# Three float32r products for the attention scores, and linear-attention products grouped by tile shape, in a two-layer trunk

## The chip, the cores and the metric

The kernel runs on one core of a Trainium2 chip. The metric is device time of one execution in microseconds (us).

## What is computed

The reference is a trunk of two layers on 256 tokens of width 1024. Each layer normalises its input, projects it, and feeds three mixers: differential attention (4 heads, two score maps each, c = 0 and 1), a state-space mixer, and gated linear attention (GLA, 4 heads, chunks of 64 tokens). Their outputs are projected and added, and a gated feed-forward part and a gated per-layer input follow. Cut to what the change touches:

```python
# differential attention, one block of 128 query rows
s = jnp.einsum('bqhcd,bkhcd->bhcqk', qi, k) * scale      # d = 64
s = jnp.where(causal, s, -jnp.inf)
pr = jax.nn.softmax(s, axis=-1)
attn = pr[:, :, 0] - lam * pr[:, :, 1]
# gated linear attention
gk = jax.nn.log_sigmoid(gate_lr @ w_gate2 + b_gate) / GLA_GATE_NORMALIZER
o_intra = jnp.einsum('bchls,bcshv->bclhv', att, vf)
states = jnp.einsum('bclhd,bclhv->bchdv', k_end, vf)     # per chunk of 64
o_inter = jnp.einsum('bclhd,bchdv->bclhv', q_dec, prev)  # prev: state before the chunk
o = rms_norm(o_intra + o_inter, g_norm) * silu(g_out)
```

All inputs and outputs are float32.

## The kernel before

Every large product is made of float32r products. `load_w` brings a weight tile by DMA into a staging buffer, rounds it on ScalarE (ACT) into a high part `wh` (L212) and subtracts on VectorE (DVE) to get the low part `wl` (L213); operands are split in the same way, and a product is high x high, high x low, low x high (`product` L225 to L227, `product_t` L237 to L245, the x units L824 to L826). The small products in the mixers have float32 operands; TensorE (PE) executes such a matmul as two records in the trace.

The work of a layer is a list of weight units. `PLAN` and `PLAN_OUT` say at which unit a generator of the mixers makes its next step: `da_gen` (differential attention), `ssd_gen` (state space), `gla_gates_gen` and `gla_gen` (GLA). The order on each engine is then set by a scheduler from priorities and dependencies. The weight units need five banks of PSUM (`bank_acc`, name acc); all mixer steps share three (`bank`, name pm). A fourth tile of pm waits until the readers of the first have ended. There are six halves of weight buffers (`NHALF`), so splits run up to three weight tiles ahead.

In `da_gen`, q and k are turned by PE transposes (L430) and copied by ACT into `qt` (L433). The scores come in three groups: the first 128 rows with 4 heads and 128 keys, and the second 128 rows with two times 2 heads and 256 keys. Each head and c has one float32 product with K = 64 (c = 0 in array rows 0 to 63, c = 1 in rows 64 to 127; L458) and then one bfloat16 product of 128 columns that adds the causal mask (L460). DVE takes the row maxima `mx` (L466), ACT the exponentials `e` (L471). The products of the state-space mixer behind the first scores are L602; DVE adds them to `xd` (L605), and the scales of L615 follow.

In GLA, `lrx` holds the low-rank gate input with a column of ones, its transpose `lrt` is multiplied with the gate weights (L694, float32). `gla_gen` forms the attention map `pa` (L726, masked into `attm` by DVE L728), turns k (L732), makes three chunk states (L744, K = 64, float32, one bank for each chunk), copies them with decay into `gst` (L757 and below), and then makes the outputs `po`: for each j, b and e one 128x128 product with `attm` (L770) and up to two 64x64 products with the states (L776). A head norm on ACT and DVE (L373 to L380), a gate (L785, writing `fyn`) and transposes (L793) follow.

Of the kernel before, what the change touches and what calls it, by code (L numbers as in the profile page):

```python
# [10 lines left out]
F32 = mybir.dt.float32  # L11
# [5 lines left out]
ALU = mybir.AluOpType  # L17
# [90 lines left out]
def trunk_kernel(ctx: ExitStack, tc: tile.TileContext, a: dict):  # L108
# [15 lines left out]
    def slot(s, dt=F32):  # L124
        return sp.tile([P, SLOT], dt, tag="slot", name=nm(s))
# [29 lines left out]
    for b in range(2):  # L155
        pool.memset(lrx[b], 0.0)
        pool.memset(lrx[b][:, 16:17], 1.0)
# [237 lines left out]
    def da_gen(i, S):  # L395
# [30 lines left out]
        for t in range(4):  # L426
            pb = bank()
            for hh in range(2):
                for b in range(2):
                    pe.transpose(pb[:, (2 * hh + b) * P:(2 * hh + b + 1) * P],  # L430
                                 qg[t][:, b * T + hh * P:b * T + (hh + 1) * P], ident)
            qt = slot("qt")
            act.activation(qt, pb, AF.Copy)  # L433
            qk.append(qt)
            if t == 1:
                yield
# [13 lines left out]
        for qb, heads in units:  # L450
            nh, nk = len(heads), P * (qb + 1)
            pb = [bank(), bank()]
            for j, hd in enumerate(heads):
                q, k = qk[hd // 2], qk[2 + hd // 2]
                o = (hd % 2) * T
                for c in range(2):
                    r = slice(64 * c, 64 * c + 64)
                    pe.matmul(pb[c][:, j * nk:(j + 1) * nk], q[r, o + qb * P:o + (qb + 1) * P],  # L458
                              k[r, o:o + nk], start=True, stop=False)
                    pe.matmul(pb[c][:, (j + 1) * nk - P:(j + 1) * nk], idb, negb, start=False, stop=True)  # L460
# [221 lines left out]
    def gla_gates_gen(i, S):  # L682

        wt = slot("w2")
        pool.dma_start(wt[:, :256], a["w2"][i])
        pl = bank()
        for b in range(2):
            pe.transpose(pl[:, b * P:(b + 1) * P], lrx[b], ident)
        lrt = slot("lrt")
# [3 lines left out]
        for b in range(2):  # L693
            pe.matmul(pg[:, b * T:(b + 1) * T], lrt[:, b * P:(b + 1) * P], wt[:, :256], start=True, stop=True)  # L694
# [19 lines left out]
    def gla_gen(i, S):  # L714
# [24 lines left out]
        pst = []  # L739
        for c in range(3):  # L740
            b, r = c // 2, slice(64 * (c % 2), 64 * (c % 2) + 64)
            pb = bank()
            for j in range(2):
                pe.matmul(pb[:, j * T:(j + 1) * T], kx[r, (2 * b + j) * P:(2 * b + j + 1) * P],  # L744
                          v[b][r, j * T:(j + 1) * T], start=True, stop=True)
            pst.append(pb)
# [16 lines left out]
        po = [bank(), bank()]  # L763
        for j in range(2):
            for b in range(2):
                o = (2 * j + b) * P
                for e in range(2):
                    hd = 2 * j + e
                    r = slice(64 * e, 64 * e + 64)
                    pe.matmul(po[e][:, o:o + P], attm[e][:, 2 * j + b], v[b][:, hd * P:(hd + 1) * P],  # L770
                              start=True, stop=True)
                    for cc in range(2):
                        c = 2 * b + cc
                        if c:
                            s = j * T + b * P + cc * 64
                            pe.matmul(po[e][64 * cc:64 * cc + 64, o:o + P], q[r, s:s + 64],  # L776
                                      prev[c][r, j * P:(j + 1) * P], start=False, stop=True,
                                      skip_group_check=True)
# [29 lines left out]
    def in_units(i, S, x):  # L808
# [45 lines left out]
        def zunit(half):  # L854
            def go(w):
# [4 lines left out]
                for b in range(2):  # L860
# [7 lines left out]
                    else:  # L868
                        dve.tensor_scalar(lrx[b][:, 0:16], pb[:, T:T + 16], rcol[:, b:b + 1], None,
                                          op0=ALU.mult)  # L870
# [234 lines left out]
def _layout(w):  # L1105
# [23 lines left out]
    w2[:, 0:16] = z["gla_w_gate2"]  # L1129
    w2[:, 16] = z["gla_b_gate"]  # L1130
# [44 lines left out]
```

## Time and profile before

| | us |
|---|---|
| median of 3 runs | 809.76 |
| lowest and highest run | 808.99, 810.79 |
| the profiled execution, device time | 808.72 |
| its span in the trace | 806.7 |
| its mean granted TensorE clock | 0.991 of full speed |
| busy: PE, DVE, ACT | 796.1, 624.6, 472.8 |

The span is the time between first and last instruction of the trace; the device time has 2 us around it. Busy time of PE counts matmuls and not weight loads (PEld), which run beside them. The granted clock is the share of full speed (2.4 GHz) that PE was given; 0.5 is 1.2 GHz. Of each timeline, the ends of matmuls are modelled, so the distance from one start to the next is what a matmul costs, and not its duration.

### The profile page before, as it was taken

How to read it: one execution, taken by the hardware profiler on the slowest of the kernel's cores; microseconds unless marked ns; L12 is line 12 of the kernel's file. 1: busy time of each engine (PE TensorE's matmuls, PEld its weight loads, DVE VectorE, ACT ScalarE, POOL GpSimd, SP SyncE). 2: the span in 40 equal slices, each digit the busy share in tenths (PEclk: the TensorE clock that was granted, in tenths of full speed). 3: DMA queues.
4: the chain of work that ended last, by engine and by line, in shares of the span. 5: the costliest groups of instructions: out<-in, count | busy, mean ns of one | idle time of the engine just before them, and what ended most of it. 6: DMA issues, size and time to landing. Idle time of an engine off the chain costs nothing.

```text
span 806.7 us, 13118 instructions
## 1 busy us (share of the span) xinstructions
PE 796.1 (99%) x5026; PEld 703.7 (87%) x5026; DVE 624.6 (77%) x1279; ACT 472.8 (59%) x820; POOL 22.8 (3%) x34
## 2 busy tenths in 40 slices
PE   8999999999999999999999999999999999999997
PEld 6998876899888888888999987778998888888897
DVE  5998977788787777667789699777888777766673
ACT  7767556556665555455667675284566566555461
POOL 2000000002000000000010000000020000000000
PEclk9999989999999999999999999899999999999999
DMA  8764331444655544557554532333445555445541
GB/s 295 278 213 140 139 103 54 157 157 158 209 164 203 188 162 144 179 182 247 207 206 163 177 112 99 107 135 124 158 160 198 197 180 206 138 153 191 196 157 53
DMA packets 24013, 134.92 MB, mean 167 GB/s; under 512 B 2960, under 2 KB 4752, under 8 KB 11408
## 3 DMA queue, kind: packets, MB, share of 16 engines
q1 hardware_dynamic: 23616, 133.57, 48.3%
q8 instruction: 39, 0.64, 0.3%
q0 software_dynamic: 192, 0.52, 0.2%
q14 instruction: 22, 0.18, 0.1%
q10 hardware_dynamic: 144, 0.01, 0.0%
HBM read 133.05 MB, written 1.05 MB: 166 GB/s over the span
## 4 chain that ended last, share of the span: by engine, by line
PE 91%; DVE 3%; ACT 2%; DMA 2%; issue 1%; SPq 0%; DVEq 0%; ACTq 0%
PE acc L237 30%; PE acc L239 15%; PE acc L245 7%; PE acc L244 7%; PE acc L243 7%; PE acc L824 4%; PE acc L825 4%; PE acc L826 4%; PE pm L458 2%; PE pm L602 1%; DMA h<-in_x 1%; PE acc L226 1%; PE acc L225 1%; PE acc L227 1%; DVE wl L213 1%
## 5 line engine op out<-in xcount | busy, mean ns | idle before, releaser
L212 ACT ACTIVATE wh<-st 128x1024 fp32r<-128x1024 f32 (+5 forms) x274 | 267.4, 979 | 234.6 <-PE acc L237 91.3
L213 DVE TENSOR_TENSOR wl<-st,wh 128x1024 fp32r<-128x1024 f32 (+5 forms) x274 | 309.3, 1132 | 105.1 <-ACT wh L212 104.8
L237 PE MATMUL acc<-x,wh 128*128 128x512 f32 x704 | 222.0, 396 | 0.1
L239 PEld LDWEIGHTS acc<-x,wl 128*128 128x128 f32 x704 | 132.3, 188 | 31.2
L239 PE MATMUL acc<-x,wl 128*128 128x256 f32 x704 | 138.4, 278 | 0.0
L237 PE MATMUL acc<-act,wh 128*128 128x512 f32 x352 | 111.8, 395 | 0.0
L237 PEld LDWEIGHTS acc<-x,wh 128*128 128x128 f32 x704 | 107.3, 189 | 0.7 <-DVE x L274 0.7
L245 PE MATMUL acc<-x,wl 128*128 128x256 f32 x320 | 90.7, 283 | 0.9 <-DVE wl L213 0.9
L243 PE MATMUL acc<-x,wh 128*128 128x256 f32 x320 | 90.9, 284 | 0.0
L244 PE MATMUL acc<-x,wh 128*128 128x256 f32 x320 | 90.5, 283 | 0.0
L239 PEld LDWEIGHTS acc<-act,wl 128*128 128x128 f32 x352 | 66.2, 188 | 14.3
L239 PE MATMUL acc<-act,wl 128*128 128x256 f32 x352 | 72.0, 279 | 0.0
L824 PE MATMUL acc<-wh,x 128*128 128x512 f32 x160 | 66.3, 417 | 0.5 <-ACT wh L212 0.5
L825 PE MATMUL acc<-wl,x 128*128 128x512 f32 x160 | 65.1, 407 | 0.0
L826 PE MATMUL acc<-wh,x 128*128 128x512 f32 x160 | 64.4, 403 | 0.0
L245 PEld LDWEIGHTS acc<-x,wl 128*128 128x128 f32 x320 | 61.2, 191 | 1.1 <-DVE wl L213 1.1
L243 PEld LDWEIGHTS acc<-x,wh 128*128 128x128 f32 x320 | 61.2, 191 | 0.2
L244 PEld LDWEIGHTS acc<-x,wh 128*128 128x128 f32 x320 | 61.2, 191 | 0.1
L237 PEld LDWEIGHTS acc<-act,wh 128*128 128x128 f32 x352 | 54.9, 189 | 1.3
L244 PE MATMUL acc<-mix,wh 128*128 128x256 f32 x192 | 54.6, 285 | 0.0
L243 PE MATMUL acc<-mix,wh 128*128 128x256 f32 x192 | 54.3, 286 | 0.0
L245 PE MATMUL acc<-mix,wl 128*128 128x256 f32 x192 | 54.1, 283 | 0.0
(259 smaller groups left out, 1167.8 us busy)
## 6 DMA issues: line engine op xcount, KB each, us to landing
st<-in_w_f SPq DMA_DIRECT2D x44, 1024.0 KB, 4.9
st<-in_w_d SPq DMA_DIRECT2D x32, 704.0 KB, 4.1
st<-in_w_x SPq DMA_DIRECT2D x18, 1024.0 KB, 4.9
st<-in_w_o SPq DMA_DIRECT2D x12, 1024.0 KB, 4.9
st<-in_w_t SPq DMA_DIRECT2D x11, 1024.0 KB, 4.9
st<-in_w_g SPq DMA_DIRECT2D x8, 1024.0 KB, 5.0
st<-in_w_z SPq DMA_DIRECT2D x3, 1088.0 KB, 5.0
st<-in_w_x SPq DMA_DIRECT2D x8, 256.0 KB, 4.8
```

The source lines that it names most:

```text
L212: i_hi = act.activation(wh[:, s], st[:, o], AF.Copy)
L213: i_lo = dve.tensor_tensor(wl[:, s], st[:, o], wh[:, s].bitcast(F32), ALU.subtract)
L225: pe.matmul(out, sh, mh, start=i == 0, stop=False)
L237: pe.matmul(out, wh[:, lo:lo + P], x[k], start=k == 0, stop=False)
L239: pe.matmul(out[:, :T], wl[:, lo:lo + P], x[k][:, :T], start=False, stop=k == n - 1)
L243: pe.matmul(out, sh, hi, start=k == 0, stop=False)
L244: pe.matmul(out, sh, x[k][:, T:], start=False, stop=False)
L245: pe.matmul(out[:, :T], sl, hi, start=False, stop=k == n - 1)
L458: pe.matmul(pb[c][:, j * nk:(j + 1) * nk], q[r, o + qb * P:o + (qb + 1) * P], k[r, o:o + nk], start=True, stop=False)
L824: pe.matmul(pb[b], xh, wh, start=kk_ == 0, stop=False)
L825: pe.matmul(pb[b], xh, wl, start=False, stop=False)
L826: pe.matmul(pb[b], xl, wh, start=False, stop=kk_ == KD - 1)
```

## The change

It does four things in each layer.

- **Scores.** q and k are kept in two parts, `qh` (ACT copy, rounded to float32r) and `ql` (DVE, what is left of the value in PSUM, 128x512, four per layer). Each head and c has three float32r products with K = 64 (high x high, high x low, low x high, c alternating inside), 48 per layer in place of 16 float32 ones. The mask is one bfloat16 product for a whole bank (6 per layer in place of 16).
- **Gates.** `lrx` holds the high part at columns 0 and 32 and the low part at 64 (and ones at 16 and 48); the gate weights are repeated at rows 0, 32 and 64, of which 32 to 63 are turned into their low part. One float32r product does what a float32 one did. It adds one ACT copy of 128x256, a DVE subtraction of 32x256, and two small DVE operations for each half of the tokens.
- **States.** The loops are exchanged: j outside, the three chunks inside, the three banks taken first.
- **Outputs.** In `po` all products with `attm` come first, then all with the states.

```diff
--- before.py
+++ after.py
@@ -154,7 +154,8 @@
     lrx = [cp.tile([P, P], F32, name=f"lrx{b}") for b in range(2)]
     for b in range(2):
         pool.memset(lrx[b], 0.0)
-        pool.memset(lrx[b][:, 16:17], 1.0)
+        for o in (16, 48):
+            pool.memset(lrx[b][:, o:o + 1], 1.0)
     attm = [cp.tile([P, 4, P], F32, name=f"attm{e}") for e in range(2)]
     for e in range(2):
         (pool if e else dve).memset(attm[e], 0.0)
@@ -429,9 +430,11 @@
                 for b in range(2):
                     pe.transpose(pb[:, (2 * hh + b) * P:(2 * hh + b + 1) * P],
                                  qg[t][:, b * T + hh * P:b * T + (hh + 1) * P], ident)
-            qt = slot("qt")
-            act.activation(qt, pb, AF.Copy)
-            qk.append(qt)
+
+            qh, ql = slot("qh", F32R), slot("ql", F32R)
+            act.activation(qh, pb, AF.Copy)
+            dve.tensor_tensor(ql, pb, qh.bitcast(F32), ALU.subtract)
+            qk.append((qh, ql))
             if t == 1:
                 yield
         yield
@@ -453,11 +456,17 @@
             for j, hd in enumerate(heads):
                 q, k = qk[hd // 2], qk[2 + hd // 2]
                 o = (hd % 2) * T
-                for c in range(2):
-                    r = slice(64 * c, 64 * c + 64)
-                    pe.matmul(pb[c][:, j * nk:(j + 1) * nk], q[r, o + qb * P:o + (qb + 1) * P],
-                              k[r, o:o + nk], start=True, stop=False)
-                    pe.matmul(pb[c][:, (j + 1) * nk - P:(j + 1) * nk], idb, negb, start=False, stop=True)
+
+                for n, (a_, b_) in enumerate(((0, 0), (0, 1), (1, 0))):
+                    for c in range(2):
+                        r = slice(64 * c, 64 * c + 64)
+                        pe.matmul(pb[c][:, j * nk:(j + 1) * nk], q[a_][r, o + qb * P:o + (qb + 1) * P],
+                                  k[b_][r, o:o + nk], start=j == 0 and n == 0, stop=False,
+                                  skip_group_check=True)
+            for c in range(2):
+
+                pe.matmul(v3(pb[c], nh)[:, :, nk - P:], idb, negb.unsqueeze(1).to_broadcast([P, nh, P]),
+                          start=False, stop=True, skip_group_check=True)
             if len(es_of) == 2:
                 attn_t(es_of[0])
             mx = small("mx", [P, 2, 4])
@@ -681,17 +690,20 @@
 
     def gla_gates_gen(i, S):
 
-        wt = slot("w2")
+        wt, wr = slot("w2"), slot("w2r", F32R)
         pool.dma_start(wt[:, :256], a["w2"][i])
+        act.activation(wr[:, :256], wt[:, :256], AF.Copy)
+        dve.tensor_tensor(wr[32:64, :256], wt[32:64, :256], wr[32:64, :256].bitcast(F32), ALU.subtract)
         pl = bank()
         for b in range(2):
             pe.transpose(pl[:, b * P:(b + 1) * P], lrx[b], ident)
-        lrt = slot("lrt")
+        lrt = slot("lrt", F32R)
         act.activation(lrt[:, :T], pl[:, :T], AF.Copy)
         yield
         pg = bank()
         for b in range(2):
-            pe.matmul(pg[:, b * T:(b + 1) * T], lrt[:, b * P:(b + 1) * P], wt[:, :256], start=True, stop=True)
+
+            pe.matmul(pg[:, b * T:(b + 1) * T], lrt[:, b * P:(b + 1) * P], wr[:, :256], start=True, stop=True)
         e = slot("ge")
         act.activation(e, pg, AF.Abs)
         act.activation(e, e, AF.Exp, scale=-1.0)
@@ -736,14 +748,12 @@
         yield
 
         v = S["gv"]
-        pst = []
-        for c in range(3):
-            b, r = c // 2, slice(64 * (c % 2), 64 * (c % 2) + 64)
-            pb = bank()
-            for j in range(2):
-                pe.matmul(pb[:, j * T:(j + 1) * T], kx[r, (2 * b + j) * P:(2 * b + j + 1) * P],
+        pst = [bank() for _ in range(3)]
+        for j in range(2):
+            for c in (0, 1, 2):
+                b, r = c // 2, slice(64 * (c % 2), 64 * (c % 2) + 64)
+                pe.matmul(pst[c][:, j * T:(j + 1) * T], kx[r, (2 * b + j) * P:(2 * b + j + 1) * P],
                           v[b][r, j * T:(j + 1) * T], start=True, stop=True)
-            pst.append(pb)
         prev = [None]
         for c in range(3):
             st = slot("gst")
@@ -761,21 +771,23 @@
             prev.append(st)
         yield
         po = [bank(), bank()]
+
         for j in range(2):
             for b in range(2):
                 o = (2 * j + b) * P
                 for e in range(2):
                     hd = 2 * j + e
+                    pe.matmul(po[e][:, o:o + P], attm[e][:, 2 * j + b], v[b][:, hd * P:(hd + 1) * P],
+                              start=o == 0, stop=False, skip_group_check=True)
+        for j in range(2):
+            for c in range(1, 4):
+                b, cc = c // 2, c % 2
+                o, s = (2 * j + b) * P, j * T + c * 64
+                for e in range(2):
                     r = slice(64 * e, 64 * e + 64)
-                    pe.matmul(po[e][:, o:o + P], attm[e][:, 2 * j + b], v[b][:, hd * P:(hd + 1) * P],
-                              start=True, stop=True)
-                    for cc in range(2):
-                        c = 2 * b + cc
-                        if c:
-                            s = j * T + b * P + cc * 64
-                            pe.matmul(po[e][64 * cc:64 * cc + 64, o:o + P], q[r, s:s + 64],
-                                      prev[c][r, j * P:(j + 1) * P], start=False, stop=True,
-                                      skip_group_check=True)
+                    pe.matmul(po[e][64 * cc:64 * cc + 64, o:o + P], q[r, s:s + 64],
+                              prev[c][r, j * P:(j + 1) * P], start=False, stop=True,
+                              skip_group_check=True)
         ys, sg = [], S["sg"]
         for e in range(2):
             yn = head_norm(po[e])
@@ -866,8 +878,12 @@
                         dve.scalar_tensor_tensor(S["dtr"][:, b], pb[:, T:T + 8], rcol[:, b:b + 1],
                                                  pr[:, O_DTB:O_DTB + 8], ALU.mult, ALU.add)
                     else:
-                        dve.tensor_scalar(lrx[b][:, 0:16], pb[:, T:T + 16], rcol[:, b:b + 1], None,
-                                          op0=ALU.mult)
+
+                        lr, hi = small("lr", [P, 16]), lrx[b][:, 0:64].rearrange("p (a c) -> p a c", a=2)
+                        dve.tensor_scalar(lr, pb[:, T:T + 16], rcol[:, b:b + 1], None, op0=ALU.mult)
+                        dve.tensor_copy(hi[:, :, 0:16].bitcast(F32R),
+                                        lr.unsqueeze(1).to_broadcast([P, 2, 16]))
+                        dve.tensor_tensor(lrx[b][:, 64:80], lr, lrx[b][:, 0:16], ALU.subtract)
                 if half == 1:
                     S["dt"], S["dta"] = ssd_dt(i, S["dtr"])
             made[f"z{half}"] = (a["w_z"][i, half], KD, 272, go)
@@ -1126,8 +1142,9 @@
     out["pos"] = pos.view(np.int32).reshape(2, P, -1).transpose(1, 0, 2)
     cw = z["ssd_conv_w"].reshape(DEPTH, 4, 8, P).transpose(0, 3, 2, 1).reshape(DEPTH, P, 32)
     w2 = np.zeros((DEPTH, P, 256), f)
-    w2[:, 0:16] = z["gla_w_gate2"]
-    w2[:, 16] = z["gla_b_gate"]
+    for r in (0, 32, 64):
+        w2[:, r:r + 16] = z["gla_w_gate2"]
+        w2[:, r + 16] = z["gla_b_gate"]
     out["par"] = np.concatenate([
         cols(z["attn_norm"], 8), cols(z["ffn_norm"], 8), cw, cols(z["ssd_conv_b"], 8),
         cols(z["ssd_norm"], 4), cols(z["gla_norm"], 1), cols(z["da_sub_norm"], 1),
```

Line numbers after the change are some 10 higher: L458 becomes L463, L460 L468, L602 L611, L744 L755, L770 L780, L776 L788, L793 L805, L728 L740, L466 L475, L605 L614, L213 L214.

The order on the engines changes more than the lines say. It is the same in both layers; the rows are those of the first.

PE, the state products (`kx`, L744 before, L755 after). Before, they stand in one piece, 24 wide projections (128x512) behind L602:

```order
L824 MATMUL acc_1412<-wh_1245,x_146 128x512
L825 MATMUL acc_1412<-wl_1246,x_146 128x512
L826 MATMUL acc_1412<-wh_1245,x_146 128x512
L744 MATMUL pm_1447<-gv_1322,kx_1268 128x256 x2
L744 MATMUL pm_1450<-gv_1322,kx_1268 128x256 x2
L744 MATMUL pm_1453<-gv_1323,kx_1268 128x256 x2
L824 MATMUL acc_1411<-wh_1327,x_156 128x512
L458 MATMUL pm_1471<-qt_1289,qt_1275 128x256
L460 LDWEIGHTS idb
L460 MATMUL pm_1471<-negb,idb 128x128
```

After, they are three pieces with projections between them, and the second scores follow at once:

```order
L838 MATMUL acc_1441<-wh_1256,x_148 128x512
L755 MATMUL pm_1476<-gv_1341,kx_1279 128x256 x2
L836 MATMUL acc_1440<-wh_1346,x_158 128x512
L837 MATMUL acc_1440<-wl_1347,x_158 128x512
L838 MATMUL acc_1440<-wh_1346,x_158 128x512
L755 MATMUL pm_1477<-gv_1341,kx_1279 128x256 x2
L836 MATMUL acc_1441<-wh_1346,x_158 128x512
L837 MATMUL acc_1441<-wl_1347,x_158 128x512
L755 MATMUL pm_1478<-gv_1342,kx_1279 128x256 x2
L463 MATMUL pm_1500<-qh_1304,qh_1286 128x256
L463 MATMUL pm_1500<-ql_1305,qh_1286 128x256
L463 MATMUL pm_1500<-qh_1304,ql_1287 128x256
```

Between the products of L602 (L611 after) and the first of them stand 24 wide projections before and 10 after; between the transposes of k (L732, L744 after) and the first scores, 17 before and 30 after. The scores of the first rows (L463) stand together, c alternating, with one of them three projections ahead of the rest; in the second rows each bank's six products and its mask stand apart, one c at a time. The first piece of L755 takes the bank that the products L611 held; what frees it is the addition to `xd` on DVE, which reads them.

DVE, up to that addition (`xd_914<-pm_1379` before, `xd_925<-pm_1408` after). Before, two weight splits (`wl`) stand between the second masking of GLA's map (`attm`) and the row maxima `mx`:

```order
L728 COPY_PREDICATED attm_87<-cst,pm_1252 128x512
L190 TENSOR_TENSOR rs_t_1168<-yf_1166 128x2
L213 TENSOR_TENSOR wl_1328<-st_1326,wh_1327 128x1024
L191 SCALAR_TENSOR_TENSOR rs_t_1168<-rs_t_1168,rs_v_1167 128x2
L213 TENSOR_TENSOR wl_1333<-st_1326,wh_1332 128x1024
L192 SCALAR_TENSOR_TENSOR yf_1166<-rs_t_1168,yf_1166 128x2
L466 TENSOR_REDUCE mx_1354<-pm_1336 128x4
L615 TENSOR_SCALAR xd_886<-xd_886,yf_1166 128x256 x2
L466 TENSOR_REDUCE mx_1354<-pm_1337 128x4
L605 TENSOR_TENSOR xd_914<-pm_1379,xd_914 128x512
L467 TENSOR_SCALAR mx_1354<-mx_1354 128x8
L213 TENSOR_TENSOR wl_1439<-st_1437,wh_1438 128x1024
```

After, four `ql` follow the masking, of which the last two are shown, and behind the scales of `xd` there are five weight splits:

```order
L436 TENSOR_TENSOR ql_1305<-pm_1299,qh_1304 128x512
L193 SCALAR_TENSOR_TENSOR yf_1177<-rs_t_1179,yf_1177 128x2
L436 TENSOR_TENSOR ql_1314<-pm_1308,qh_1313 128x512
L624 TENSOR_SCALAR xd_897<-xd_897,yf_1177 128x256 x2
L214 TENSOR_TENSOR wl_1347<-st_1345,wh_1346 128x1024
L214 TENSOR_TENSOR wl_1352<-st_1345,wh_1351 128x1024
L214 TENSOR_TENSOR wl_1468<-st_1466,wh_1467 128x1024
L214 TENSOR_TENSOR wl_1473<-st_1466,wh_1472 128x1024
L214 TENSOR_TENSOR wl_1563<-st_1561,wh_1562 128x1024
L475 TENSOR_REDUCE mx_1383<-pm_1355 128x4
L475 TENSOR_REDUCE mx_1383<-pm_1356 128x4
L614 TENSOR_TENSOR xd_925<-pm_1408,xd_925 128x512
```

The five splits have moved ahead of the maxima of the scores, and the addition to `xd` stands behind both.

PE, the output products of GLA. Before, the two kinds alternate over both banks (`pm_1681` and `pm_1682`), in eight rounds:

```order
L770 MATMUL pm_1681<-gv_1322,attm_86 128x128
L776 MATMUL pm_1681<-gst_1456,gq_760 64x128
L770 MATMUL pm_1681<-gv_1323,attm_86 128x128
L776 MATMUL pm_1681<-gst_1461,gq_760 64x128
L770 MATMUL pm_1682<-gv_1322,attm_87 128x128
L776 MATMUL pm_1682<-gst_1456,gq_760 64x128
```

After, each bank has four products with `attm` and then six with the states (here from the third):

```order
L780 MATMUL pm_1722<-gv_1341,attm_88 128x128
L780 MATMUL pm_1722<-gv_1342,attm_88 128x128
L788 MATMUL pm_1722<-gst_1485,gq_768 64x128
L788 MATMUL pm_1722<-gst_1490,gq_768 64x128
L788 MATMUL pm_1722<-gst_1495,gq_768 64x128
```

The second bank follows 17 projections of 256 columns later. Behind the products of the second bank, 45 projections stand ahead of the transposes of its normed rows (L805); before, 67 stood ahead of them.

## Rows read from the trace of the kernel before

**Rows 1.** The page, part 1: busy time and share of the span per engine.

```profile
PE 796.1 (99%) x5026; PEld 703.7 (87%) x5026; DVE 624.6 (77%) x1279; ACT 472.8 (59%) x820; POOL 22.8 (3%) x34
```

**Rows 2.** Busy by stretch: span, then PE, PEld, DVE, ACT, POOL busy, PEclk, DMA, GB/s.

```profile
57.00:80.00 23.00, 22.00 (x134) 19.16 (x133) 20.90 (x44) 16.38 (x23) 0.10 (x1) 1.00 0.47 161
80.00:104.00 24.00, 24.00 (x155) 20.79 (x154) 22.79 (x70) 13.43 (x24) 0.00 (x0) 1.00 0.36 127
104.00:109.15 5.15, 5.15 (x33) 3.46 (x31) 4.18 (x9) 2.81 (x5) 0.00 (x0) 1.00 0.17 19
109.15:116.00 6.85, 6.85 (x26) 6.08 (x26) 4.74 (x9) 2.56 (x15) 0.00 (x0) 0.50 0.34 139
505.10:512.00 6.90, 6.90 (x27) 6.05 (x27) 4.53 (x9) 1.96 (x11) 0.00 (x0) 0.51 0.37 141
```

**Rows 3.** Timeline of PE, first scores: start us, duration us, instructions (xcount).

```profile
105.03 0.48 PE L458 MATMUL pm<-qt,qt 64*128 64x128 f32 x2
...
109.03 3.51 PE L602 MATMUL pm<-xdt,m 128*128 128x64 f32 x16
```

**Rows 4.** Timeline of PE, state products and second row block's scores.

```profile
119.12 0.39 PE L825 MATMUL acc<-wl,x 128*128 128x512 f32 x1
119.35 0.39 PE L826 MATMUL acc<-wh,x 128*128 128x512 f32 x1
119.67 1.99 PE L744 MATMUL pm<-gv,kx 64*128 64x256 f32 x12
121.59 0.50 PE L824 MATMUL acc<-wh,x 128*128 128x512 f32 x1
122.02 0.70 PE L458 MATMUL pm<-qt,qt 64*128 64x256 f32 x2
...
123.48 0.48 PE L825 MATMUL acc<-wl,x 128*128 128x512 f32 x1
...
130.57 0.70 PE L458 MATMUL pm<-qt,qt 64*128 64x256 f32 x2
...
132.90 0.61 PE L445 MATMUL pm<-cst,e 128*128 128x128 f32 x4
```

**Rows 5.** Timeline of PE, output products of the linear attention.

```profile
145.72 0.38 PE L770 MATMUL pm<-gv,attm 128*128 128x128 f32 x2
...
147.16 0.49 PE L770 MATMUL pm<-gv,attm 128*128 128x128 f32 x2
147.58 0.43 PE L776 MATMUL pm<-gst,gq 64*64 64x128 f32 x4
147.95 0.49 PE L770 MATMUL pm<-gv,attm 128*128 128x128 f32 x2
...
151.86 0.65 PE L445 MATMUL pm<-cst,e 128*128 128x128 f32 x4
```

**Rows 6.** Timeline of PE, two projections of 256 columns.

```profile
156.06 0.28 PE L226 MATMUL acc<-pl,wh 128*128 128x256 f32 x1
156.18 0.28 PE L227 MATMUL acc<-ph,wl 128*128 128x256 f32 x1
```

**Rows 7.** Groups by line and form: gate product, busy us and mean ns.

```profile
L694 PE MATMUL pm<-w,lrt 128*128 128x256 f32 x8 | 2.1, 378 | 0.0
```

**Rows 8.** Timeline of DVE around the first scores; in brackets idle before, releaser.

```profile
104.48 0.75 DVE L728 COPY_PREDICATED attm<-cst,pm 128x512 f32<-128x512 uint32 x1
...
105.16 1.24 DVE L213 TENSOR_TENSOR wl<-st,wh 128x1024 fp32r<-128x1024 f32 x1
106.30 0.18 DVE L191 SCALAR_TENSOR_TENSOR rs_t<-rs_t,rs_v 128x2 f32<-128x2 f32 x1
...
109.27 0.61 DVE L615 TENSOR_SCALAR xd<-xd,yf 128x256 f32<-128x256 f32 x2
...
112.58 0.69 DVE L605 TENSOR_TENSOR xd<-pm,xd 128x512 f32<-128x512 f32 x1 [2.11 <-PE pm L602]
```

**Rows 9.** Waits of PE: line, released by, us in total, times, longest.

```profile
PE pm L793 <- DVE fyn L785: 0.7, 2, 0.3
```

## The prediction

> **What bounds the kernel.** I read the page's busy times first: PE is busy for 796.1 of 806.7 us, so there is hardly a wait to remove, and any gain must be PE work that goes away [rows 1]. The second view is the busy time by stretch, around the mixers of the first layer [rows 2]. It shows two more things. DVE has little room ahead of the first scores: 2.1 us idle in 57 to 80 and 1.2 us in 80 to 104. And right behind the first scores of each layer PE is granted 0.5 of its clock, 1.2 GHz, for 6.85 us (109.15 to 116) and 6.9 us (505.1 to 512). PE was busy for all 5.15 us ahead of the first fall, so it fell behind short products and not behind an idle engine. At half speed such a stretch costs about 3.4 us. The third view is the timeline, of PE for prices and of DVE for who comes late.
>
> **PE work per layer.** Prices are distances between starts.
>
> *Scores of the first rows.* Before: from 105.03 to 109.03, 4.0 us [rows 3]. After: 24 products of 128 columns and two masks of 512. No row shows a float32r product with K = 64 or under 256 columns; one of 256 columns costs 0.12 us [rows 6], so at most that, unless short ones are priced like float32. The float32 products show that the halves of the array can work side by side: the state products before are twelve records in 1.92 us [rows 4], where two records of 256 columns in a gate product mean 0.52 us (four products in 2.1 us of two layers [rows 7]), so twelve in a row would need 3.1. Here c alternates, so I take twelve pairs at 0.11, 1.3 us, the masks at 0.23 each as a 512-column projection [rows 4], and 0.5 for three changes of the tile's shape (the first projection behind the state products starts 0.43 us ahead of the next work in place of 0.23, so up to 0.2 each [rows 4]). That is 2.3 us, a gain of **1.7**. Without pairs it is 24 x 0.12 = 2.9 and a total of 3.9: a gain of 0.1. At a float32-like price in pairs (0.21, half of a 256-column float32 product) the total is 3.5, a gain of 0.5; with neither, 6.0, a loss of 2.0. I take pairs because the trace shows them for these same row halves.
>
> The Trainium skill (TensorE: Matmul & The Clock Gate, "Back-to-back issue gap") gives some 81 ns for a weight load and a product of 128 columns. By that figure 24 in a row would take 1.9 us and the block 2.9, a gain of 1.1; no row here shows such a pair.
>
> *Scores of the second rows.* Before: four blocks, 1.46 us for the first (122.02 to 123.48) and 2.33 for the last two together (130.57 to 132.90); with the second like the first, 5.25 us [rows 4]. After: four blocks of six products of 256 columns of one c, one after the other, 0.72 us, a mask of 256 columns at 0.12 and 0.25 for two changes of shape: 1.1 each, 4.4 together. Gain **0.9**, bounds 0.6 to 1.4 (0.1 us per product).
>
> *States.* Before: one piece, 119.67 to 121.59, 1.92 us [rows 4]. After: three pieces with projections between, each of two float32 products at 0.43 to 0.52 and a change of shape of 0.1 to 0.2, some 1.05; no two chunks are side by side any more. Loss **1.2**, bounds 0.9 to 1.4.
>
> *Outputs of GLA.* Before: eight rounds of two kinds in 6.14 us, 145.72 to 151.86 [rows 5]. A round is 0.42 for the product with `attm` (147.16 to 147.58) and 0.37 for those with the states, where four records take no longer than one pair would: two tiles are side by side. Half of each, some 0.2, is the change of shape, since a float32 product of 128 columns is half of one of 256 (0.21 us). After: per bank 0.42 + 3 x 0.21 for the first kind and 0.37 + 3 x 0.21 for the second (six products, of which four find a partner), 2.05; two banks 4.1. Gain **1.9**, bounds 1.1 (no partners) to 2.2.
>
> *Gates.* Before: two products, half of 2 x 2.1 / 4, so 1.05 us of records per layer, in start distances some 0.85 [rows 7]. After: 2 x 0.12. Gain **0.6**.
>
> The sum is 1.7 + 0.9 - 1.2 + 1.9 + 0.6 = **3.9 us per layer**.
>
> **What comes late instead.** DVE gets four `ql` per layer, and they stand just where it is full. Count it from the second masking of `attm` at 104.48 [rows 8]; I take this time as unchanged, because the gates' additions (a 128x256 copy's worth and four tiny operations for two halves, about 1 us) fit into the 3.3 us of idle time in 57 to 104. The masking and a small operation take 0.68 (104.48 to 105.16). Then four `ql` of the same size, 2.7; the scales, 0.6; five weight splits at 1.14 (105.16 to 106.30), 5.7; two maxima and the addition to `xd` at 0.69 [rows 8], 2.1. The addition ends at 116.3. Before, DVE was done with two splits and idle for 2.1 us in front of this addition (112.58), waiting for PE.
>
> PE gets there sooner. The scores begin at 105.03 - 0.6 for the gates + 13 x 0.23, since 30 projections in place of 17 stand ahead: 107.4. The block ends at 109.7, the eight products L611 take 1.7 (half of the 3.51 us that their sixteen records took at half clock [rows 3]), ten projections 2.3. PE is at the first state product at 113.7. That product needs the bank which the addition frees at 116.3, and everything on PE is queued behind it, projections that are ready too: a **new wait of 2.2 to 2.6 us per layer**; I take 2.2, since a duration on DVE exceeds the distance to the next start by 0.1 (1.24 against 1.14), which the last three operations have in them. A dearer score product does not change the end: it eats into this wait.
>
> Smaller ones: the second transposes of `fyn` have 22 projections less ahead, 2.6 us of cover, where they waited for 0.3 us already [rows 9]; its chain no longer starts behind the first bank's, so 0 to 2.9, I take 0.5. The gate product and the first score products have one more copy or subtraction ahead: 0 to 0.6, I take 0.25. The ACT copies of the gate weights and `qh` (in place of `qt`) lie beside PE work, with ACT busy for 16.4 of 23 us and 13.4 of 24 [rows 2]; the GpSimd memsets are at the start. Together 0.75.
>
> Per layer 3.9 - 2.2 - 0.75 = 0.95, for two layers **1.9 us less**, if the half-clock stretches stay as many as they are. Then the profiled execution's 808.72 becomes 806.8. The median of the runs is 1.04 above that execution, so I forecast **807.9 us**.
>
> **Rivals.** A measurement tells about 0.2%, 1.6 us, from no change.
>
> - *The clock stays up* or falls where it hides the wait. The score block shrinks from 4.0 to 2.3 us, so less short work stands in one place; without both falls another 6.8 us go: 801.1. If it falls behind the scores as before, PE reaches the state products some 2.5 us later, the wait is gone, and 4.4 us go: 803.5. For it: the shorter block. Against it: short products L611 still follow, and then PE stands idle. Chance 0.25.
> - *The clock falls once more in each layer* (slower). The place is the first state product: PE idle for 2.2 us, and then a float32 piece on half of the array, behind a fall at the scores that remains, or with a further one at the outputs, where PE also has a short wait. Each costs 3.4 us. Two of them make -1.9 + 6.8 = +4.9, so 814.7; it decides from the first of them on (-1.9 + 3.4 = +1.5). For it: the trace has falls behind short work alone. Against it: a fall at the scores shortens the wait. Chance 0.28. The Trainium skill (TensorE: Matmul & The Clock Gate, "HAM oscillation") has idle waits of PE bring the clock down; the two falls of this trace came without any, so the trace does not bear it out and does not exclude it.
> - *DVE keeps up*: the splits are not late, say because they start sooner. Then the 4.4 us of waits do not come, 803.5, or with no falls 796.7. Chance 0.05: the splits' place ahead of the addition is fixed in the queue.
> - *The products do not pair* or are priced like float32. Then PE arrives later, and the wait takes most of it: the loss is 0 to 2 us per layer at worst, 808 to 812. It is part of the forecast's own spread.
>
> **How the numbers follow.** The forecast has 0.42, with its own range of 805 to 812; the rivals 0.25, 0.28 and 0.05. The forecast lies 1.9 under the median, just outside what can be told, so I split it: half faster, a third the same, the rest slower. Faster: 0.21 + 0.25 + 0.04 = 0.5, cut to 0.48 for the rival whose fall hides the wait only in one layer; same 0.17; slower 0.07 + 0.28 = 0.35. The range goes from 800.5 (no falls, with pairs) to 816 (two more falls, and a little).
>
> **What would show it.** Right: the scores of the first rows take some 2.3 us, the outputs 4.1, a DVE-released wait of 2 us or more at the first state product in both layers, its splits packed without a gap from 105 to 115, and two half-clock stretches. The forecast is wrong if PE does not wait there, if a stretch with a granted clock of 0.5 is missing or a third one appears, or if the score products cost over 0.2 us each.

## The result, and the profile after

| | before | after |
|---|---|---|
| median of 20 runs, us | 807.87 | 814.66 |
| lowest and highest run, us | 802.80, 810.79 | 808.83, 816.86 |
| profiled execution, us (span) | 808.72 (806.7) | 808.83 (806.7) |
| busy PE, DVE, ACT in it, us | 796.1, 624.6, 472.8 | 787.6, 629.9, 473.0 |

The ratio after to before is 1.0074, with a 95% interval of 1.0055 to 1.0093: the change made the kernel slower by some 6 us (6.8 by the medians). The forecast was 807.9, a little faster than the 809.76 that it started from; what came is the time of the rival on the other side, 814.7. In three of the experiments below one execution took 2.0 to 4.4 ms; these three are left out of every figure.

The executions of one kernel differ by how much time they spend at half clock. Before, over the executions of all sessions, they lie between 802.3 us at a mean granted clock of 1.000 and 810.9 at 0.989, most often near 809 at 0.991. After, seven lie between 808.8 and 810.4 (0.988 to 0.991), ten between 814.2 and 815.4 (0.982) and three between 816.5 and 816.9 (0.980 or 0.981). A span times its mean clock is roughly the time without half clock: 800.3 x 1.000 = 800 for the shortest span of before, 807.0 x 0.991 = 800 for a common one; 806.7 x 0.991 = 799 and 812.7 x 0.982 = 798 after. So at full clock both kernels take the same time within 2 us, and the 6 us are half clock. The profile after is of the fastest of its 20 executions, so it shows less half clock than most had: about as much as the profile before.

PE did get less to do: it is busy for 8.5 us less in a span of the same length. First, PE's timeline after, at the places that the sum of the forecast names (gate products, first scores, first state products, second scores, one bank of outputs; start, duration, instructions):

```profile
62.81 0.40 PE L706 MATMUL pm<-w2r,lrt 128*128 128x256 f32 x2
63.05 0.28 PE L638 MATMUL pm<-sdta,cst 128*128 128x8 f32 x2
...
108.46 0.38 PE L463 MATMUL pm<-qh,ql 64*128 64x128 f32 x2
108.58 0.38 PE L463 MATMUL pm<-qh,qh 64*128 64x128 f32 x2
...
110.22 1.90 PE L611 MATMUL pm<-xdt,m 128*128 128x64 f32 x16
...
116.54 1.10 PE L755 MATMUL pm<-gv,kx 64*128 64x256 f32 x4 [2.07 <-DVE mx L476]
117.56 0.50 PE L836 MATMUL acc<-wh,x 128*128 128x512 f32 x1
...
120.96 0.47 PE L463 MATMUL pm<-qh,qh 64*128 64x256 f32 x1
...
121.98 0.48 PE L838 MATMUL acc<-wh,x 128*128 128x512 f32 x1
...
142.60 1.05 PE L780 MATMUL pm<-gv,attm 128*128 128x128 f32 x8
143.58 1.08 PE L788 MATMUL pm<-gst,gq 64*64 64x128 f32 x12
144.60 0.39 PE L226 MATMUL acc<-ph,wh 128*128 128x256 f32 x1
```

The score products of the first rows go in pairs 0.11 to 0.12 us apart, the first block of second scores takes 1.02 us, the first piece of state products 1.02, a bank of outputs 2.0, the gates 0.24. These answer to [rows 3, 4, 5, 7].

Then the waits of PE (in all, times, longest). The first and third are new (`ple` is the projected per-layer input, which ACT copies out of PSUM); the second answers to [rows 9].

```profile
PE pm L755 <- DVE mx L476: 4.1, 2, 2.1
PE pm L805 <- DVE fyn L797: 3.2, 2, 1.6
PE acc L244 <- ACT ple L915: 1.5, 2, 0.8
```

What the first waits for is on DVE's timeline, from the last `ql` to the operation behind the addition to `xd` (L614). It answers to [rows 8]:

```profile
107.70 0.69 DVE L436 TENSOR_TENSOR ql<-pm,qh 128x512 fp32r<-128x512 f32 x1
108.31 0.60 DVE L624 TENSOR_SCALAR xd<-xd,yf 128x256 f32<-128x256 f32 x2
108.84 5.76 DVE L214 TENSOR_TENSOR wl<-st,wh 128x1024 fp32r<-128x1024 f32 x5
114.51 1.28 DVE L475 TENSOR_REDUCE mx<-pm 128x4 f32<-128x512 f32 x2
115.71 0.68 DVE L614 TENSOR_TENSOR xd<-pm,xd 128x512 f32<-128x512 f32 x1
116.31 0.16 DVE L476 TENSOR_SCALAR mx<-mx 128x8 f32<-128x8 f32 x1
```

DVE does not rest; five splits in a row hold up the maxima and the addition, which ends at 116.31, the very time that the forecast counted (116.3). The trace puts the wait down to L476, the operation behind it.

Last the stretches (span, busy PE, PEld, DVE, ACT, POOL, PEclk, DMA share, GB/s), in place of [rows 2]:

```profile
109.00:116.00 7.00, 5.47 (x43) 4.49 (x41) 7.00 (x8) 1.19 (x3) 0.00 (x0) 1.00 0.53 180
...
503.00:511.60 8.60, 6.54 (x36) 4.97 (x35) 7.51 (x11) 2.20 (x13) 0.00 (x0) 1.00 0.68 244
511.70:521.90 10.20, 10.20 (x27) 7.25 (x27) 6.77 (x28) 3.27 (x11) 0.00 (x0) 0.50 0.01 2
556.06:559.48 3.42, 3.42 (x18) 3.42 (x17) 2.29 (x6) 1.87 (x4) 0.00 (x0) 0.50 0.59 249
```

No fall stands right behind the first scores any more, in neither layer (they end at 110 and 503), where both were before. The two that this execution has in its layers are in the second one, the first some 2 us behind the wait at the state products (which ended at 509.5) and the other 0.5 us behind the wait at the transposes of `fyn` (at 555.5). They cost (10.2 + 3.4) / 2 = 6.8 us, as much as the two of before. In the first layer the same waits stood and the clock held. In most executions there must have been more falls, since 0.982 means 14.6 us lost to half clock (812.7 x 0.018) and 0.991 means 7.3; where they stood, no profile shows.

### The profile page after: what moved, and what is told of

It reads as the page before. It is cut to its first block, busy times and chain, and to the rows that moved or that the text cites. A ratio compares the mean times of both kernels' runs of the same rounds, so it can differ in the third digit from the quotient of the medians.

```text
span 806.7 us, 13158 instructions
## 1 busy us (share of the span) xinstructions
PE 787.6 (98%) x5034; PEld 701.5 (87%) x5034; DVE 629.9 (78%) x1297; ACT 473.0 (59%) x822; POOL 22.8 (3%) x36
## 3 DMA queue, kind: packets, MB, share of 16 engines
HBM read 133.05 MB, written 1.05 MB: 166 GB/s over the span
## 4 chain that ended last, share of the span: by engine, by line
PE 86%; DVE 8%; ACT 2%; DMA 2%; issue 1%; SPq 0%; ACTq 0%; DVEq 0%
PE acc L238 30%; PE acc L240 15%; PE acc L246 8%; PE acc L245 7%; PE acc L244 7%; PE acc L836 3%; PE acc L838 3%; PE acc L837 2%; DVE wl L214 2%; PE acc L226 1%; PE acc L227 1%; PE acc L228 1%; DMA h<-in_x 1%; PE pm L755 1%; PE pm L463 1%
## 5 line engine op out<-in xcount | busy, mean ns | idle before, releaser
L213 ACT ACTIVATE wh<-st 128x1024 fp32r<-128x1024 f32 (+5 forms) x274 | 267.1, 979 | 233.6 <-PE acc L238 91.7
L214 DVE TENSOR_TENSOR wl<-st,wh 128x1024 fp32r<-128x1024 f32 (+5 forms) x274 | 307.8, 1129 | 108.5 <-ACT wh L213 108.1
```

Of the source, the lines that this page charges most:

```text
L213: i_hi = act.activation(wh[:, s], st[:, o], AF.Copy)
L214: i_lo = dve.tensor_tensor(wl[:, s], st[:, o], wh[:, s].bitcast(F32), ALU.subtract)
```

## The experiments

The theory after this: the subtractions and the new order make DVE late at two places; PE stands idle there, and the clock falls behind the idle time. The rivals: the short products cost more, or bring the clock down themselves; the grouped outputs are at fault; DVE is simply too full.

**One part at a time.** Scores alone (gates, states, outputs as before), and the three GLA edits alone.

> The score part alone; gates, states and outputs as before. Theory (late DVE work lets PE stand idle, and the clock falls behind the idle time): in this order only four splits stand ahead of the addition to xd, 1.14 us less, and 13 projections in place of 10 stand ahead of the state products, so the wait at the state products is under 1 us per layer, no stretch of half clock follows it, and the time is 800 to 805 us, below before. Rival (the float32r products with K = 64 are dear themselves): 810 us or more, with over 0.2 us from one score product to the next.

> Gates, states and outputs changed, scores as before. Theory: without the ql subtractions DVE's order around the scores is that of before, so PE does not wait at the state products; the work removed (1.9 for outputs, 0.6 for gates per layer) makes it some 5 us faster than before, with the same two half-clock stretches behind the scores: 800 to 805 us. Rival (the grouped outputs cost the time, by a wait at the transposes of the normed rows): 2 us or more of that wait and no gain over before.

Scores alone: 806.3 us, ratio 0.9991 (0.9966 to 1.0017), no difference that can be told and a little over what the theory gave. GLA alone: 804.65, 0.9977 (0.9953 to 1.0002), 3.3 us less by the medians and at the edge of what can be told; in its profile PE does not wait for `fyn`, so the grouped outputs alone are not at fault. So neither part is slow by itself, and the loss comes from both together. The score part was run once more for its profile:

> The score part alone once more, for its profile: under 1 us of wait at the state products per layer, score products in pairs 0.11 us apart, and half-clock stretches, if any, behind short products and not behind a wait.

It took 805.96 us, in a single execution. At the state products PE waits there for the exponentials on ACT, 1.4 us in four waits, and not for DVE. Its half clock stands behind the state products and in front of and beside the second scores:

```profile
118.60:125.30 6.70, 6.70 (x20) 5.33 (x20) 6.11 (x26) 0.97 (x2) 0.00 (x0) 0.50 0.08 16
514.55:517.90 3.35, 3.35 (x12) 2.71 (x11) 3.32 (x16) 0.72 (x1) 0.00 (x0) 0.50 0.03 12
```

So in this execution the clock fell where there were short products and waits of 0.4 us at most; GLA alone has its falls behind the scores, as before. That much the rival on short products has right.

**The splits held at the first place.** Three of the five splits are made to follow the addition to `xd`:

```diff
-                i_lo = dve.tensor_tensor(wl[:, s], st[:, o], wh[:, s].bitcast(F32), ALU.subtract)
+                with ExitStack() as es:
+                    for ins in held:
+                        es.enter_context(tc.issue_after(ins))
+                    i_lo = dve.tensor_tensor(wl[:, s], st[:, o], wh[:, s].bitcast(F32), ALU.subtract)
...
+    held = []
...
-                dve.tensor_reduce(mx[:, c, :nh], v3(pb[c], nh), AX.X, ALU.max)
+                i_mx = dve.tensor_reduce(mx[:, c, :nh], v3(pb[c], nh), AX.X, ALU.max)
+            if qb == 0:
+                held[:] = [i_mx.ins]
...
-            dve.tensor_tensor(y, py, y, ALU.add)
+            i_add = dve.tensor_tensor(y, py, y, ALU.add)
+            if b == 1:
+                held.append(i_add.ins)
```

> The change with one difference: three of the five weight splits are held behind the maxima and the addition to xd on DVE. Theory: the addition ends 3.4 us sooner, the wait of 4.1 us at the state products goes, and with it the half-clock stretch behind it: 803 to 807 us, 8 us or more below the change. Rival (the clock falls behind the short products whatever PE waits for): the wait goes, half-clock stretches stay at or near the state products, and the time is 810 us or more.

It took 802.7 us, 0.9959 (0.9938 to 0.9980) of before and 12 us under the change, a little under what the theory gave. The waits of PE:

```profile
PE pm L813 <- DVE fyn L805: 4.4, 2, 2.2
...
PE pm L763 <- ACT e L486: 0.5, 2, 0.3
```

and DVE there:

```profile
108.97 2.35 DVE L217 TENSOR_TENSOR wl<-st,wh 128x1024 fp32r<-128x1024 f32 x2
111.25 1.28 DVE L479 TENSOR_REDUCE mx<-pm 128x4 f32<-128x512 f32 x2
112.44 0.68 DVE L620 TENSOR_TENSOR xd<-pm,xd 128x512 f32<-128x512 f32 x1
113.04 0.16 DVE L482 TENSOR_SCALAR mx<-mx 128x8 f32<-128x8 f32 x1
```

The addition ends at 113.04 in place of 116.31, and the wait of 4.1 us at the state products (L763 here) is gone. Its executions lie at 801.4 to 803.6 us, with clocks of 0.993 to 0.995. Half clock is left behind the other wait alone (157.3 to 160.7 and 549.8 to 553.2, some 1 us behind its end), which has grown to 4.4 us.

**Held at both places.** What makes that other wait is seen in the changed kernel, in the second head norm on DVE:

```profile
152.86 0.16 DVE L193 SCALAR_TENSOR_TENSOR ff<-rs_t,ff 128x4 f32<-128x4 f32 x1
153.81 1.23 DVE L214 TENSOR_TENSOR wl<-st,wh 128x1024 fp32r<-128x1024 f32 x1 [0.79 <-ACT wh L213]
154.95 0.15 DVE L191 TENSOR_TENSOR rs_t<-ff 128x4 f32<-128x4 f32 x1
155.02 1.22 DVE L214 TENSOR_TENSOR wl<-st,wh 128x1024 fp32r<-128x1024 f32 x1
156.16 0.15 DVE L192 SCALAR_TENSOR_TENSOR rs_t<-rs_t,rs_v 128x4 f32<-128x4 f32 x1
```

Two splits stand inside the chain of small operations that makes `fyn`: 0.79 us of waiting for ACT and 2.3 us of splitting, in a chain that PE waits for. The next kernel lets the later splits follow the chain too (`held[:]` is set to the last gate of L797).

> The change with the splits held at two places: behind the addition to xd as in the run before, and behind the second head norm of the linear attention, so that the two splits inside its chain (2.4 us) go behind it. Theory: the remaining wait of 4.4 us at the transposes of the normed rows shrinks by at least 2 us and the half-clock stretches behind it (3.4 us each) go: 795 to 800 us. Rival (DVE is simply full there): the pushed splits come late, PE waits for wl for 2 us or more per layer instead, and the time is 802 us or more.

It took 793.4 us: 0.9835 of before (0.9796 to 0.9874), 14 us faster than the kernel before and 21 than the change, under what the theory gave. Neither wait is left: at the state products 0.5 us in two waits remain, and the waits of PE that are longer (0.9 us at most behind the start of the program) stand elsewhere and in the kernel before or in the change too. There is no half clock in it but at the very end of the program. Its four executions lie within 0.7 us, at 0.999 or 1.000.

```profile
100.00:130.00 30.00, 29.52 (x171) 23.01 (x172) 28.94 (x85) 16.49 (x42) 0.00 (x0) 1.00 0.31 106
130.00:170.00 40.00, 39.98 (x305) 37.11 (x304) 33.85 (x93) 24.58 (x46) 0.00 (x0) 1.00 0.38 131
490.00:530.00 40.00, 39.73 (x232) 31.23 (x230) 35.80 (x98) 26.47 (x64) 0.00 (x0) 1.00 0.31 108
530.00:570.00 40.00, 39.97 (x336) 39.15 (x335) 35.14 (x91) 20.35 (x34) 0.00 (x0) 1.00 0.45 156
```

DVE is busy for 28.94 of 30 us and PE is idle for only 0.5: DVE was not too full, its order was wrong. The span is 16.0 us shorter than that of the change's profile: 4.1 + 3.2 for the two waits, 1.5 for the wait for `ple`, which is gone too, and 6.8 for the half clock make 15.6.

**Held at the second place alone, and the holds on the kernel before.**

> The change with the splits held at the second place alone (behind the second head norm). Theory: the wait of 4.1 us at the state products and the half clock behind it stay, the wait at the transposes (3.2 us) and what follows it go: 804 to 811 us, between the change (814.7) and the fifth run (793.4). Rival (one cause only, the second place): 796 us or less.

> The kernel before with the splits held at the same two places as in the fifth run. Theory (the holds only mend what the change's subtractions and new order did): around the first scores DVE's order is that of before, the wait at the transposes of the normed rows was 0.7 us in all, so at most 1 us is gained and half clock stays behind the scores: 802 to 809 us, unclear against before. Rival (the holds are the gain, the change adds nothing): 798 us or less.

The second place alone: 807.52 us, within what the theory gave. The first wait is whole, and this is what follows it in the first layer of its profile:

```profile
PE pm L759 <- DVE mx L480: 4.1, 2, 2.1
```

```profile
117.20:130.80 13.60, 13.60 (x34) 9.34 (x33) 7.19 (x29) 4.92 (x19) 0.00 (x0) 0.50 0.12 32
```

In its second layer the same wait stood and no half clock followed it. The hold at the first place is thus worth 14 us more on top of the second (807.5 to 793.4), of which only 4.1 is the wait itself. The holds on the kernel before gave 808.9, 0.9997 (0.9967 to 1.0027): they are worth nothing there, and its half clock behind the scores stays (107.9 to 118.2 and 507.3 to 514.1). So the gain of the 793.4 us is the change's, once DVE's order lets it have it.

The product of span and mean clock splits each time in two, averaged over the executions: what the kernel takes at full clock, and what half clock adds. (One execution of before is left out, whose clock of 0.946 does not fit its time.)

| | at full clock, us | half clock adds, us |
|---|---|---|
| before | 799.7 | 5.1 |
| the change | 798.4 | 12.8 |
| held at the first place | 795.3 | 4.7 |
| held at the second place | 794.7 | 9.9 |
| held at both | 790.8 | 0.2 |

Between the last two rows lie 3.9 us at full clock, which is the wait, and 9.7 us of half clock. So where the splits stand decides both. That it is the idle time itself that brings the clock down is argued from this and not shown: no run has the wait's length without its idleness.

**What did not go as expected.** Three runs were to tell the wait from the clock, and the subtractions from the order.

Fill: nine unused 512-column products ahead of the state products.

```diff
+FILL = 9
...
+        fill = bank_acc()
+        for _ in range(FILL):
+            pe.matmul(v3(fill, 4), idb, negb.unsqueeze(1).to_broadcast([P, 4, P]), start=True, stop=True)
         pst = [bank() for _ in range(3)]
```

> The change with nine mask-like products of 512 columns whose result is not used, put ahead of the state products, where PE waits; DVE's late addition stays. They take 2 us of the 2.1 that PE waits. Theory: the wait's own time is still spent, but the engine is not idle, so no half clock follows it: 805 to 810 us, mean granted clock 0.988 or more in most runs. Rival (the loss is the wait alone, the clock falls for another reason): 813 to 816 us with the same half-clock stretch behind the state products.

It took 815.06 us, within what the rival gave, but the order changed with it: the state products came in one piece, and PE now waited inside it for the exponentials.

```profile
PE pm L809 <- DVE fyn L801: 4.0, 2, 2.0
PE pm L759 <- ACT e L481: 3.3, 4, 0.9
```

The wait was moved, not filled, and the one for `fyn` grew from 3.2 to 4.0 us, so the run does not tell the two apart.

No subtraction (`qk.append((qh, qh))`: the low parts are left out, the products keep their number):

> The change without the ql subtractions: the low parts of q and k are left out and all three score products take the high parts, so PE has the same number of products. Theory: DVE has 2.7 us less and one split less ahead of the addition to xd, PE does not wait at the state products, and no half clock follows: 797 to 804 us. Rival (the short score products or the shape changes bring the clock down): 808 us or more, half-clock stretches right behind the scores.

It took 807.36 us, between what the theory and what the rival gave. PE does not wait for the addition, but elsewhere for DVE: for the copies of the states, whose banks the second scores need, and for `fyn`.

```profile
PE pm L462 <- DVE gst L766: 3.6, 2, 1.8
PE pm L804 <- DVE fyn L796: 3.0, 2, 1.5
```

A split stands in front of the first of these copies on DVE:

```profile
117.58 1.23 DVE L214 TENSOR_TENSOR wl<-st,wh 128x1024 fp32r<-128x1024 f32 x1
118.71 0.17 DVE L187 TENSOR_SCALAR yf<-rs_v 128x2 int32<-128x2 int32 x1
118.78 0.41 DVE L766 COPY gst<-pm 64x256 f32<-64x256 f32 x1
```

Behind each of the four waits there is a half-clock stretch of 3.4 us, and none right behind the scores of the first rows. Two of the four begin where a block of second scores has followed the wait, so this run does not part the wait from the short products. The kernel before with the subtractions added and not used:

> The kernel before with the four subtractions added per layer and their result not used; scores as before. In this order only two splits stand ahead of the addition to xd, so it ends at about 113, before PE (some 116). Theory (it is the five splits ahead of the addition, with the subtractions, not the subtractions alone): no wait at the state products, within 2 us of before. Rival (the subtractions alone are too much for DVE): a wait of 2 us per layer there and 812 us or more.

It took 819.33 us, 1.0151 (1.0102 to 1.0200), far outside. No wait at the state products, as the order said, but `fyn` was late again, by 4.4 us (0.7 before):

```profile
PE pm L794 <- DVE fyn L786: 4.4, 2, 2.2
```

The same two splits stand in the chain that makes it, with more idle time in front of them than in the change:

```profile
160.04 1.23 DVE L213 TENSOR_TENSOR wl<-st,wh 128x1024 fp32r<-128x1024 f32 x1 [1.56 <-ACT wh L212]
...
161.26 1.22 DVE L213 TENSOR_TENSOR wl<-st,wh 128x1024 fp32r<-128x1024 f32 x1
```

It has four stretches of half clock of some 6.8 us, two behind the scores and two that begin some 1 us before this wait ends (at 163.6 and 566.3). So the subtractions upset the order at a place far from them, and a mere 2.7 us of DVE work per layer can cost 11 us. The theory is right on the splits' order and was too narrow on where it bites: not one place, but each of the three found here where a split lands in a chain that PE waits for.

**Do c = 0 and c = 1 need to alternate?** The kernel of 793.4 us with the three products of c = 0 ahead of those of c = 1:

```diff
-                for n, (a_, b_) in enumerate(((0, 0), (0, 1), (1, 0))):
-                    for c in range(2):
+                for c in range(2):
+                    for n, (a_, b_) in enumerate(((0, 0), (0, 1), (1, 0))):
```

> The fifth run's kernel with the three products of c = 0 ahead of the three of c = 1 for each head, the same products in another order. Theory (c = 0 and c = 1 run side by side on the two row halves): of 24 products of the first rows only neighbours of different c still overlap, so they take some 16 to 18 steps of 0.11 us in place of 12: 0.4 to 0.7 us per layer, 794 to 795 us, more only if half clock appears behind the longer block. Rival (they never overlap, 0.06 us each): no difference, 793.4 us.

It took 793.35 us, no difference, though not as the rival had it: the products still go in pairs. The order on PE is the scheduler's, and it was not read for this run; so the run shows that the order in the source does not matter, and not what unpaired products would cost.

```profile
107.65 0.32 PE L467 MATMUL pm<-ql,qh 64*128 64x128 f32 x1
107.65 0.32 PE L467 MATMUL pm<-qh,qh 64*128 64x128 f32 x1
107.81 0.27 PE L467 MATMUL pm<-qh,ql 64*128 64x128 f32 x1
107.82 0.27 PE L467 MATMUL pm<-ql,qh 64*128 64x128 f32 x1
```

## Why the prediction was wrong

**The step that failed** is the last of the sum: "if the half-clock stretches stay as many as they are". In the profiled execution they are as many, but their places moved from behind the scores to behind the new waits; and in most executions there is twice as much half clock (14.6 us of loss against 7.3 in the most frequent executions before). On the average it adds 12.8 us in place of 5.1, which is more than the whole loss. What could have told: the forecast had already found a wait of 2.2 us in each layer and then costed it as its own length alone. The runs show what it costs on top: with it 807.5, without it 793.4. It also kept two things that by its own working do not go together: the whole wait, which PE meets only when the clock holds behind the scores, and the two stretches of before, which stood there. For the stretches it named no other place.

**The rival's number is right in part by luck.** Two more stretches of 3.4 us gave 814.7, and the median is 814.66. It had a chance of 0.28, less than the forecast's 0.42. Its kind of cause is what the runs show, half clock behind the new waits. But its price was 4.9 us on top of 809.76, the median of three runs; from the median of twenty, 807.87, the change cost 6.8; and in the profile no stretch remained behind the scores.

**The second term that was mis-sized** is the transposes of `fyn`: 0.5 us per layer, bounds 0 to 2.9; measured 1.6 in place of 0.3. The forecast looked at PE's cover and at the first bank's chain, and not at what had moved into the second chain on DVE. Two waits are in no term of it: 0.75 per layer for `ple` on ACT, and 0.35 for `qg` on DVE.

**What held.** The new wait at the state products: 2.07 us against 2.2, with the addition's end to the tenth, though the parts of that count are off and cancel: the `ql` began at 105.56 in place of 105.16, and the maxima and the addition took 1.8 in place of 2.1; PE came at 114.5 in place of 113.7. The first scores: from 108.30 to 110.22, 1.9, with the one product that stands ahead some 2.2, against 2.3; the pairs and their 0.11 too. The second scores, 1.02 a block against 1.1, so 4.1 against 4.4. States, 1.02 for the first piece against 1.05. Outputs, 2.0 a bank against 2.05. Gates, 0.24 against 0.24. The work removed, 3.9 us per layer in the forecast, comes to some 4.8 by these distances (1.8 + 1.2 - 0.9 + 2.1 + 0.6; the third piece of the states was 0.8). (For the outputs the forecast's own numbers, 6.14 and 4.1, give a gain of 2.0 and not 1.9.) The new waits come to some 4.2 per layer (2.07 + 1.3 + 0.75 + 0.35, less 0.25 saved at the wait for `conv` on ACT) in place of 2.95. Both errors nearly cancel: at full clock the change is 1.3 us faster, where the forecast had 1.9.

**The rival on DVE keeping up** was at 803.5, or 796.7 with no half clock; the kernel with both holds makes its condition true, at 793.4. The Trainium skill (TensorE: Matmul & The Clock Gate, "HAM oscillation") has idle waits bring the clock down. The runs agree in the main: 10.2 us at half clock after the wait at 509.5, 13.6 us in the run with the second hold alone, none once both waits are gone. It is not the whole of it, since the falls of the kernel before stand behind scores without a wait, and the clock held behind some of the same waits.

## What to carry to other kernels

A wait on the engine that bounds the kernel can cost more than its length. In the profiles here a half-clock stretch came with 13 of the 16 waits of 1.5 to 2.2 us that PE has in the mixers: so count each such new wait with a stretch behind it, as the likely case and not the rival. When a change adds work to a second engine that is nearly full, read that engine's new order for long operations that are not urgent (here weight splits) in front of short ones that the first engine waits for; a part that gains nothing may need only that order mended. And run the parts together only with an eye on that order: each of these two was neutral or better alone.

## What was not expected of the hardware

Products on the two row halves of the array overlap, 0.11 us from one pair to the next, whichever of the two orders the source has. In the run with c = 0 ahead of c = 1 a product with `qh` alone and one with a `ql` start together at 107.65. Whether the scheduler put them side by side or the engine started one ahead of another is not shown. Two float32r products of 128 columns with K = 64, a price that no row showed before the change, take 0.11 us together, no more than one of 256 columns with K = 128 (0.12).

What stays open: why in one execution the clock falls behind a wait and in the next it holds behind the same one (the first layer of the profile after), and so how to tell ahead of time which of two places will be hit.
